# Attention products grouped by array mode: masks ahead of both halves, a mask as contraction rows, 64x64 products in runs

## The chip, the cores and the metric

The kernel runs on one core of a Trainium2 chip. The metric is device time in microseconds (us); a kernel's time is the median of its runs. TensorE (PE in the rows) multiplies, VectorE (DVE), ScalarE (ACT) and GpSimd (POOL) work on vectors, and SyncE (SP) issues the loads.

## The reference

A network of two kinds of layer, two layers of each, on 256 tokens of width 1024. A layer of the first kind has a feed-forward part, a token mixer with three branches (retention, latent attention, differential attention), cross attention to 256 memory tokens, and a second feed-forward part. A layer of the second kind has a mixer of stick-breaking attention and gated linear attention, and then 32 experts of which each token uses two. The parts that the change touches, cut to their products:

```python
# latent attention, 8 heads of 64 + 32; a query sees the chunks of 64 keys up to its own
sc = (einsum('bqhd,bkhd->bhqk', qn, k_nope) + einsum('bqhd,bkd->bhqk', qr, k_rope)) * scale
p = masked_softmax(sc, chunk_causal_mask(i, s))
# differential attention, 4 heads with two halves j of 64
sc = einsum('bqhjd,bkhjd->bhjqk', qb, k) * scale
p = masked_softmax(sc, chunk_causal_mask(i, s))
w = p[:, :, 0] - lam * p[:, :, 1]
# stick-breaking attention, 8 heads of 64, strictly causal
z = einsum('bhqd,bhkd->bhqk', q_blk, k) * scale
log_fail = where(before, -softplus(z), 0.0)
w = where(before, exp(log_sigmoid(z) + suffix_sum(log_fail)), 0.0)
# gated linear attention, 4 heads (64 wide keys, 128 wide values), chunks of 64
intra = einsum('bhnqk,bhnkv->bhnqv', where(causal, q_dec @ k_inv.T, 0.0), vc)
chunk_kv = einsum('bhnkd,bhnkv->bhndv', kc * exp(b_last - b), vc)
inter = einsum('bhnqd,bhndv->bhnqv', q_dec, prev)     # prev: the state before the chunk
```

## The kernel before

Tokens lie in two tiles of 128. Weights stream from memory in raw chunks of 1 MB and are split on ScalarE (line 272, the high half) and VectorE (line 274, the low half) into operands of one pass each; a dense product (mm3, lines 284 to 286) multiplies high by high, high by low and low by high, 512 columns at a time. Attention products instead take 32-bit operands as they are, and TensorE runs each of these as two passes.

Dense work and attention are interleaved by hand. The function dense emits six products for one k-tile and then calls tick, which lets the first task of each of two queues emit its next piece. A task is a generator that yields for how many ticks its next piece may wait. TensorE, ScalarE, VectorE and GpSimd run in the order in which the program is written; SP's loads alone are placed by a scheduler. PSUM has six banks for products (mm) and two for transposes and small results (tp).

In mix (the mixer of the first kind), heads_T transposes latent queries and keys into qT and kT, tiles of 128 rows of which 96 are used. latent_pairs takes two heads at a time: chunk_scores (lines 751 to 756) first multiplies two rows of constants, mrow, which puts a large negative number on the masked scores, and then adds the scores of queries 0 to 127 on keys 0 to 127 and of queries 128 to 255 on all keys. softmax2 follows, and weights_T transposes the result a few ticks later. diff_heads calls chunk_scores for the two halves j of a head; half j lies in rows 64 j to 64 j + 63 of dT. Retention (ret_pairs, lines 1041 and 1042) multiplies two heads in the same layout without a mask: both products of j = 0 are written first, then both of j = 1.

In mix2, stick works on two heads at a time. For each half j, line 1504 puts the mask in PSUM by multiplying the identity with maskb, and lines 1505 and 1506 add the scores, of 64 contraction rows. ScalarE then takes Abs (line 1509), Exp (1510) and Ln (1511), VectorE adds (1513), and three ticks after the scores TensorE sums over keys (1518, 1519); two Exp (1522) and the product with the values (1493, 1494) follow. attention runs stick on three pairs, then linear, then the fourth pair. linear multiplies queries and keys (line 1546), makes the chunks' key-value products (kv, line 1557) one chunk per tick, updates the states S on VectorE, and then writes the output go head by head: the product within a tile (line 1575, 128 rows) and then those with the states (line 1579, 64x64). Eight squares on ScalarE (437), copies (1587), a power on GpSimd (406) and a scaling (1591) follow.

Of the kernel before, what the change touches and what calls it, by code (L numbers as in the profile page):

```python
# [13 lines left out]
BF16 = mybir.dt.bfloat16  # L14
# [44 lines left out]
def constants():  # L59
# [13 lines left out]
    mrow = np.zeros((1, 512), np.float32)  # L73
    mrow[0, :64] = 1.0
    mrow[0, 128 + 64:128 + 128] = NEG
    mrow[0, 128 + 320:128 + 384] = NEG
    c["mrow"] = mrow
    same = (i[:, None] // CHUNK) == (i[None, :] // CHUNK)
# [81 lines left out]
class Stream:  # L160
    """The weights in the order of their use: loads run ahead as far as the raw buffers go, the splits into
    (hi, lo) as far as the split buffers go."""
# [21 lines left out]
    def slot(self, i):  # L184
        """the place of the next split, from raw i, or None"""
# [53 lines left out]
class Kernel:  # L239
# [8 lines left out]
    # ---------------------------------------------------------------- helpers  # L248
# [19 lines left out]
    def split(self, place, raw, c0, n, pool=False):  # L268
        """(hi, lo) of n <= 512 columns"""
        nc = self.nc  # L270
        hi, lo = place[:, :n], place[:, 512:512 + n]
        nc.scalar.activation(hi, raw[:, c0:c0 + n], AF.Copy)  # L272
        eng = nc.gpsimd if pool else nc.vector
        eng.tensor_tensor(out=lo, in0=raw[:, c0:c0 + n], in1=hi.bitcast(F32), op=ALU.subtract)  # L274
        return hi, lo
# [12 lines left out]
    # tasks are generators that emit a piece of work and yield for how long (in steps of dense) the next may wait  # L288
# [39 lines left out]
    def dense(self, keys, kt, n, lhs, outs, mid=None):  # L328
        """outs[t] ([128, n <= 512] in PSUM) = lhs @ w; the chunks of the weights hold kt k-tiles of n columns."""
# [12 lines left out]
    def staggered(self, keys, lhs):  # L342
        """run(t), for t = 0 and then 1, gives outs[t] = lhs @ w for two chunks of 4 k-tiles of 512 columns"""
# [19 lines left out]
    def dense_out(self, keys, lhs, tail, closing=None, mid=(), ada=None):  # L363
        """y[t][half] ([128, 512] in PSUM), chunks of 2 k-tiles of 1024 columns, and a function that emits what is
        left to do for t = 1 in the last tail splits"""
# [32 lines left out]
    def rstd(self, out, ms, eps=EPS, mul=1.0):  # L398
        """out = (mul * ms + eps) ** -0.5"""
# [13 lines left out]
    def new_h(self):  # L413
        """(hi, lo) of a feature-major operand [128, tile, 8, 128]"""
# [3 lines left out]
    def to_fm_g(self, src, dst, nk):  # L418
        """dst = (hi, lo) [128, nk, 128] of the transposes of src [128, nk * 128]"""
# [19 lines left out]
    def rstd2(self, out, ms, eps=EPS):  # L439
        """out = (ms[0] + ms[1] + eps) ** -0.5"""  # L440
# [17 lines left out]
    def pre_load(self, pre):  # L458
        """gain and shift"""
# [7 lines left out]
    def add_post(self, y, t, post, g, u, junk):  # L467
        """x += the normalised or gated y (two halves of 512 columns), in two steps"""
# [40 lines left out]
    def boundary(self, ys, rest, post, gp, gn, first=None, filler=None):  # L509
        """adds the last stage's output to x and gives the next stage's normalised input, feature-major, and the  # L510
        outputs of the next stage's first projection"""
# [52 lines left out]
    # ---------------------------------------------------------------- setup  # L564
# [33 lines left out]
    def setup_rope(self):  # L598
# [3 lines left out]
        self.mrow = cp.tile([1, 512], BF16, name="mrowb")  # L602

        yield 0
        with self.tc.tile_pool(name="ropew", bufs=1) as wp:
            mrow = self.A1("mrow")[0:1, 0:512]
# [37 lines left out]
    # ---------------------------------------------------------------- FFN  # L644
# [12 lines left out]
    def vectors_of(self, l, which):  # L657
        """the modulation vectors (layer, number) that are made beside an FFN"""
# [46 lines left out]
    # ---------------------------------------------------------------- token mixing  # L705
    def rope(self, x, heads, si, rot, tmpp):
        """rotates the first rot columns of the heads x [128, tile, heads, width] in place"""
# [15 lines left out]
    def evacuate(self, dst, ps):  # L723
        """dst [128, 2, 512] = both tiles of ps"""
# [3 lines left out]
    def copy(self, dst, src):  # L728
        """on the scalar and the vector engine in turn"""
# [6 lines left out]
    def transposes_g(self, dst, blocks, rows=128):  # L736
        """dst [rows, n, 128] = transposes of the n blocks [128, rows]"""
# [13 lines left out]
    def chunk_scores(self, ps, qf, kf):  # L751
        """ps [128, 384]: queries 0-127 on keys 0-127, queries 128-255 on keys 0-255, chunk-causal"""
        te = self.nc.tensor
        te.matmul(ps[:, 0:384], self.mrow[:, 0:128], self.mrow[:, 128:512], start=True, stop=False)
        te.matmul(ps[:, 0:128], qf(0, 128), kf(0, 128), start=False, stop=False)
        te.matmul(ps[:, 128:384], qf(128, 256), kf(0, 256), start=False, stop=True)

    def softmax2(self, ps, P, scale, sm):
        """P = exp(scale * (ps - max)) for two score sets ps[j] [128, 384]; returns 1 / sums [128, 4] (set, tile)"""
# [15 lines left out]
    def weights_T(self, P, wp):  # L775
        """[128 keys, 384] = (keys 0-127 x queries 0-255 | keys 128-255 x queries 128-255) of P [128, 384]"""
# [8 lines left out]
    def attend_tm(self, pt, v, h, o):  # L785
        """o [128, 2, 128] in PSUM = weights @ v for the queries of both tiles"""
# [6 lines left out]
    def branch_fm(self, o, wp):  # L793
        """(hi, lo) [128, 4, 256] of o [128, 2, 512], appended to out"""
# [6 lines left out]
    def head_norms(self, o_tp, o, ms, h):  # L801
        """o (SBUF) and its mean squares from PSUM o_tp [128, 2, 128]"""
# [15 lines left out]
    def mix(self, l, hT, ps, pre):  # L818
# [7 lines left out]
        with ExitStack() as es:  # L826
# [23 lines left out]
            # latent attention: norms  # L850
# [26 lines left out]
            # differential attention: scalars  # L877
# [9 lines left out]
            # latent attention: queries  # L887
# [16 lines left out]
            def heads_T(dst, src, name):  # L904
                for t in range(2):
# [8 lines left out]
            # latent attention: keys and values  # L914
# [21 lines left out]
            def latent_pairs():  # L936
                last = None
                for hp in range(5):
                    if hp < 4:
                        ps = self.mm("msc")  # L940
                        for j in range(2):
                            h = 2 * hp + j
                            self.chunk_scores(ps[j], lambda c0, c1: qT[:96, h, c0:c1], lambda c0, c1: kT[:96, h, c0:c1])
# [24 lines left out]
            # differential attention  # L968
            branch = {0: (mh, ml)}

            def diff_heads():
# [11 lines left out]
                for h in range(5):  # L983
                    if h < 4:
                        ps = self.mm("dsc")
                        for j in range(2):
# [1067 lines left out]
```

## Time and profile before

| what | before |
|---|---|
| median of 3 runs | 2297.43 us |
| lowest and highest run | 2295.17, 2300.14 us |
| span of the profiled execution | 2296.8 us |
| TensorE busy | 2161.8 us (94%) |
| VectorE, ScalarE busy | 1338.2 us (58%), 1084.0 us (47%) |
| first mixer's latent to differential scores, layers 1 and 2 | 279 to 362, 1047 to 1130 us |
| second mixer's stick and linear part, layers 1 and 2 | 1607 to 1668, 1979 to 2040 us |

The profile records one execution; of it only the span, from the first to the last instruction, is given. A busy share is an average over all stages, so the stretches around the edited places are read on their own. A record of TensorE has a start and a modelled end; since products are pipelined, ends overlap, and the distance between starts tells what one costs.

### The profile page before, as it was taken

To read this page: it belongs to the slowest core of one execution; us is meant where nothing else is said; L and a number is where in the kernel's file an instruction comes from. 1 tells how busy PE (TensorE), PEld (TensorE's weight loads), DVE (VectorE), ACT (ScalarE), POOL (GpSimd) and SP (SyncE) were. 2 spreads that over 40 slices of the span, in tenths; PEclk is the share of its full clock that TensorE was granted. 3 is DMA by queue.
4 is the path that set the end of the run, shared out by engine and by line. 5 is a ranking of instruction groups with operands and counts; after the bars stand their busy time and mean duration, and the time that the engine had idled before them with its cause. 6 is when DMAs were issued, how large, how long until landed. Compare 5 with 4: busy or idle time off the path is not lost. (4 is left out here: it accounts for less than half of the span.)

```text
span 2296.8 us, 28925 instructions
## 1 busy us (share of the span) xinstructions
PE 2161.8 (94%) x10684; PEld 1584.9 (69%) x10684; DVE 1338.2 (58%) x2419; ACT 1084.0 (47%) x2178; POOL 121.2 (5%) x115
## 2 busy tenths in 40 slices
PE   7999999999999999999999999999989877998885
PEld 6887877888787787777788878877764334765341
DVE  6876666765876777676678567766461115453111
ACT  5544666565544555466656555445641103752110
POOL 1001000000100100010000010002010001001000
PEclk9999999999999999999999999999989898998998
DMA  8865434553676676653345447766389998558998
GB/s 291 300 242 209 178 125 151 196 198 129 211 279 236 218 277 242 234 196 129 145 181 202 160 141 277 240 231 242 116 316 393 420 419 316 197 202 327 419 418 338
DMA packets 96230, 559.27 MB, mean 244 GB/s; under 512 B 11135, under 2 KB 13105, under 8 KB 43086
## 3 DMA queue, kind: packets, MB, share of 16 engines
q1 hardware_dynamic: 96078, 557.30, 65.5%
q8 instruction: 88, 1.44, 0.2%
q14 instruction: 64, 0.52, 0.1%
HBM read 556.16 MB, written 1.10 MB: 243 GB/s over the span
## 5 line engine op out<-in xcount | busy, mean ns | idle before, releaser
L274 DVE TENSOR_TENSOR hl<-raw,hl 128x512 fp32r<-128x512 f32 (+2 forms) x586 | 391.6, 684 | 122.7 <-ACT hl L272 115.5
L272 ACT ACTIVATE hl<-raw 128x512 fp32r<-128x512 f32 (+1 forms) x602 | 367.3, 628 | 198.7 <-PE gu L286 49.6
L274 DVE TENSOR_TENSOR pair<-raw,pair 128x512 fp32r<-128x512 f32 (+2 forms) x468 | 304.8, 692 | 127.4 <-ACT pair L272 122.5
L272 ACT ACTIVATE pair<-raw 128x512 fp32r<-128x512 f32 x484 | 276.9, 623 | 186.2 <-PE gu L286 70.3
L1898 PE MATMUL gu<-raw,xg 128*32 128x512 f32 x1024 | 142.1, 626 | 25.4 <-DMA raw<-w_gu 25.4
L284 PE MATMUL gu<-hl,hh 128*128 128x512 f32 x320 | 127.6, 399 | 0.0
L284 PE MATMUL gu<-pair,hh 128*128 128x512 f32 x320 | 127.5, 398 | 0.0
L286 PE MATMUL gu<-hl 128*128 128x512 f32 x320 | 126.5, 395 | 0.0
L285 PE MATMUL gu<-hl,hh 128*128 128x512 f32 x320 | 126.1, 394 | 0.0
L286 PE MATMUL gu<-pair,hl 128*128 128x512 f32 x320 | 125.1, 391 | 0.0
L285 PE MATMUL gu<-pair,hh 128*128 128x512 f32 x320 | 124.8, 390 | 0.0
L1295 DVE SCALAR_TENSOR_TENSOR ada<-raw,cact,ada 128x512 f32<-128x512 f32 x168 | 121.9, 745 | 0.0
L1898 PEld LDWEIGHTS gu<-raw,xg 128*32 128x32 f32 x1024 | 29.2, 111 | 101.8 <-DMA raw<-w_gu 52.7
L1886 PEld LDWEIGHTS gather<-P,u 128*128 128x128 f32 x512 | 71.5, 219 | 32.6 <-issue 23.5
L279 DVE TENSOR_TENSOR y<-dn,y 128x512 fp32r<-128x512 f32 x32 | 22.1, 692 | 110.4 <-ACT y L278 110.4
L1937 ACT ACTIVATE sil<-gu 128x256 f32<-128x256 f32 x16 | 6.1, 384 | 163.2 <-PE gu L1898 163.2
L443 POOL TENSOR_TENSOR rs<-rs_tmp,mhalf 128x1 f32<-128x1 f32 x44 | 25.6, 583 | 1081.0 <-DVE rs_tmp L442 1075.8
L1955 PE MATMUL dn<-raw,aT 128*32 128x512 f32 x512 | 73.5, 621 | 8.9 <-DVE aT L1947 3.6
L1886 PE MATMUL gather<-P,u 128*128 128x128 f32 x512 | 78.6, 310 | 1.6 <-DVE P L1874 1.6
L1938 DVE SCALAR_TENSOR_TENSOR sil<-sil,cs,gu 128x256 f32<-128x256 f32 x16 | 7.7, 480 | 121.3 <-ACT sil L1937 121.1
L284 PE MATMUL y<-hl,ah 128*128 128x512 f32 x184 | 72.6, 395 | 0.0
L284 PEld LDWEIGHTS gu<-pair,hh 128*128 128x128 f32 x320 | 60.1, 188 | 17.0 <-ACT pair L272 2.5
(670 smaller groups left out, 4776.8 us busy)
## 6 DMA issues: line engine op xcount, KB each, us to landing
raw<-w SPq DMA_DIRECT2D x131, 1024.0 KB
raw<-w_gu SPq DMA_DIRECT2D x98, 1024.0 KB
raw<-win SPq DMA_DIRECT2D x71, 1024.0 KB
raw<-w_dn SPq DMA_DIRECT2D x54, 1024.0 KB
raw<-w_ada SPq DMA_DIRECT2D x48, 1024.0 KB
raw<-w_gu SPq DMA_DIRECT2D x60, 512.0 KB
raw<-w_out SPq DMA_DIRECT2D x16, 1024.0 KB
raw<-cross_wkv SPq DMA_DIRECT2D x16, 1024.0 KB
```

Of the source, the lines that this page charges most:

```text
L272: nc.scalar.activation(hi, raw[:, c0:c0 + n], AF.Copy)
L274: eng.tensor_tensor(out=lo, in0=raw[:, c0:c0 + n], in1=hi.bitcast(F32), op=ALU.subtract)
L279: self.nc.vector.tensor_sub(lo, src, hi.bitcast(F32))
L284: te.matmul(out, xh, wh, start=start, stop=False)
L285: te.matmul(out, xh, wl, start=False, stop=False)
L286: te.matmul(out, xl, wh, start=False, stop=stop)
L443: self.nc.gpsimd.tensor_tensor(out=out, in0=tmp, in1=self.mhalf[:, 0:1], op=ALU.pow)
L1295: nc.vector.scalar_tensor_tensor(self.ada[:, c], w, act, self.ada[:, c], op0=ALU.mult, op1=ALU.add)
L1886: te.matmul(ps[:, (k - k0) * 128:(k - k0 + 1) * 128], hm[t][:, k * 128:(k + 1) * 128], P[t][:, q * 128:(q + 1) * 128], start=(t == 0), sto ...
L1898: te.matmul(gu[32 * e:32 * e + 32, :], xg[:, k, 32 * e:32 * e + 32], w(e), start=(k == 0), stop=(k == 7))
L1938: ve.scalar_tensor_tensor(sil, sil, cs[:, q:q + 1], gu[:, 256:512], op0=ALU.mult, op1=ALU.mult)
L1955: te.matmul(dn[half][32 * e:32 * e + 32, :], aT[:, f, 32 * e:32 * e + 32], w(e), start=(f == 0), stop=(f == 1))
```

## The change

Four things change. The latent mask becomes two more contraction rows: a constant mqk is loaded into rows 96 and 97 of qT and kT, the products have 98 rows, and no mask product is left. For differential attention, chunk_mask writes the masks of both halves first, over the masked columns alone, and the scores of both halves follow; the columns without a mask are not started first. In stick the masks of both halves stand first too, over 256 columns where it were 384. In linear, the key-value products of chunks 0 and 1 are emitted together, and the output has the eight products of 128 rows first and then the twelve of 64x64. The changed kernel also has comments and docstrings taken out, so its line numbers differ.

```diff
-    def chunk_scores(self, ps, qf, kf):
+    def chunk_mask(self, ps):
+        out = ps.rearrange("p (a b) -> p a b", a=2)[:, :, 64:128]
+        self.nc.tensor.matmul(out, self.mrow[:, 0:128], self.mrow[:, 128:256].rearrange("p (a b) -> p a b", a=2),
+                              start=True, stop=True)
+
+    def chunk_scores(self, ps, qf, kf, masked):
         te = self.nc.tensor
-        te.matmul(ps[:, 0:384], self.mrow[:, 0:128], self.mrow[:, 128:512], start=True, stop=False)
-        te.matmul(ps[:, 0:128], qf(0, 128), kf(0, 128), start=False, stop=False)
-        te.matmul(ps[:, 128:384], qf(128, 256), kf(0, 256), start=False, stop=True)
+        te.matmul(ps[:, 0:128], qf(0, 128), kf(0, 128), start=not masked, stop=True, skip_group_check=masked)
+        te.matmul(ps[:, 128:384], qf(128, 256), kf(0, 256), start=not masked, stop=True, skip_group_check=masked)
...
             def heads_T(dst, src, name):
+                rows = a["mqk"][("qT", "kT").index(name)].rearrange("r (h n) -> r h n", h=8)
+                nc.sync.dma_start(dst[96:98], rows)
...
-                            self.chunk_scores(ps[j], lambda c0, c1: qT[:96, h, c0:c1], lambda c0, c1: kT[:96, h, c0:c1])
+                            self.chunk_scores(ps[j], lambda c0, c1: qT[:98, h, c0:c1], lambda c0, c1: kT[:98, h, c0:c1],
+                                              False)
...
                         for j in range(2):
+                            self.chunk_mask(ps[j])
+                        for j in range(2):
                             r = slice(64 * j, 64 * j + 64)
-                            self.chunk_scores(ps[j], lambda c0, c1: dT[r, h, c0:c1], lambda c0, c1: dT[r, 4 + h, c0:c1])
+                            self.chunk_scores(ps[j], lambda c0, c1: dT[r, h, c0:c1], lambda c0, c1: dT[r, 4 + h, c0:c1],
+                                              True)
...
-        self.maskb = cp.tile([128, 384], BF16, name="maskb")
+        self.maskb = cp.tile([128, 128], BF16, name="maskb")
...
-        nc.gpsimd.memset(self.maskb, 0.0)
...
                 for j in range(2):
+                    te.matmul(ps[j].rearrange("p (a b) -> p a b", a=2)[:, :, 0:128], self.identb,
+                              self.maskb.unsqueeze(1).to_broadcast([128, 2, 128]), start=True, stop=True)
+                for j in range(2):
                     r = slice(64 * j, 64 * j + 64)
                     q, k = qk[r, hp, :], qk[r, 4 + hp, :]
-                    te.matmul(ps[j][:, 0:384], self.identb, self.maskb, start=True, stop=False)
-                    te.matmul(ps[j][:, 0:256], k[:, 0:128], q, start=False, stop=False)
-                    te.matmul(ps[j][:, 256:384], k[:, 128:256], q[:, 128:256], start=False, stop=True)
+                    te.matmul(ps[j][:, 0:256], k[:, 0:128], q, start=False, stop=True, skip_group_check=True)
+                    te.matmul(ps[j][:, 256:384], k[:, 128:256], q[:, 128:256], start=False, stop=True,
+                              skip_group_check=True)
...
+            kvs = []
             for c in range(3):
-                t, r = c // 2, slice(64 * (c % 2), 64 * (c % 2) + 64)
-                kv = self.tp("kv")
-                for hp in range(2):
-                    te.matmul(kv[:, hp * 256:(hp + 1) * 256], ex[2][r, t, hp * 128:(hp + 1) * 128],
-                              gv[r, t, hp * 256:(hp + 1) * 256], start=True, stop=True)
+                if c != 1:
+                    for c2 in ((0, 1), (2,))[c // 2]:
+                        t, r = c2 // 2, slice(64 * (c2 % 2), 64 * (c2 % 2) + 64)
+                        kvs.append(self.tp("kv"))
+                        for hp in range(2):
+                            te.matmul(kvs[c2][:, hp * 256:(hp + 1) * 256], ex[2][r, t, hp * 128:(hp + 1) * 128],
+                                      gv[r, t, hp * 256:(hp + 1) * 256], start=True, stop=True)
+                kv = kvs[c]
...
             for t in range(2):
                 for h in range(4):
-                    cs = slice(h * 128, (h + 1) * 128)
-                    j, pl = h % 2, place(t, h)
-                    te.matmul(ps[j][:, pl], sc[:, j, pl], gv[:, t, cs], start=True, stop=True)
-                    for c in (2 * t, 2 * t + 1):
-                        if c:
-                            r = slice(64 * (h % 2), 64 * (h % 2) + 64)
-                            te.matmul(ps[j][64 * (c % 2):64 * (c % 2) + 64, pl], qki[r, h // 2, c * 64:(c + 1) * 64],
-                                      S[r, h // 2, c - 1, :], start=False, stop=True, skip_group_check=True)
+                    te.matmul(ps[h % 2][:, place(t, h)], sc[:, h % 2, place(t, h)], gv[:, t, h * 128:(h + 1) * 128],
+                              start=(t == 0 and h < 2), stop=True, skip_group_check=True)
+            for hp in range(2):
+                for c in range(1, 4):
+                    for j in range(2):
+                        r, pl = slice(64 * j, 64 * j + 64), place(c // 2, 2 * hp + j)
+                        te.matmul(ps[j][64 * (c % 2):64 * (c % 2) + 64, pl], qki[r, hp, c * 64:(c + 1) * 64],
+                                  S[r, hp, c - 1, :], start=False, stop=True, skip_group_check=True)
```

TensorE's order at the first differential head: dsc is the bank of a half (two numbers, two halves), gate the dense product around it. Before:

```order
L286 MATMUL gate_2794<-hl 128x512
L754 LDWEIGHTS mrowb
L754 MATMUL dsc_2904<-mrowb 128x384
L755 MATMUL dsc_2904<-dT 128x128
L756 MATMUL dsc_2904<-dT 128x256
L754 LDWEIGHTS mrowb
L754 MATMUL dsc_2905<-mrowb 128x384
L755 MATMUL dsc_2905<-dT 128x128
L756 MATMUL dsc_2905<-dT 128x256
L284 MATMUL gate_2934<-hl,hh 128x512
```

And of the change:

```order
L290 MATMUL gate_2788<-hl 128x512
L759 LDWEIGHTS mrowb
L759 MATMUL dsc_2898<-mrowb 128x2x64
L759 LDWEIGHTS mrowb
L759 MATMUL dsc_2899<-mrowb 128x2x64
L765 MATMUL dsc_2898<-dT 128x128
L766 MATMUL dsc_2898<-dT 128x256
L765 MATMUL dsc_2899<-dT 128x128
L766 MATMUL dsc_2899<-dT 128x256
L288 MATMUL gate_2928<-hl,hh 128x512
```

The second half's mask has moved ahead of the first half's scores, so the four products of 64 rows stand together; stick-breaking pairs changed in the same way.

SP's order at the first mixer's start; gm and dl are its small constants, win, wq_b and wkv_b its weights. Before:

```order
L848 DMA dl<-dlam 128x256
L410 DMA gain<-g_mix 128x1024
L265 DMA raw<-win 128x2048 x2
L410 DMA gain<-g_cross 128x1024
L265 DMA raw<-wq_b 128x1536
L265 DMA raw<-win 128x2048 x2
L265 DMA raw<-wkv_b 128x1024
```

And of the change:

```order
L858 DMA dl<-dlam 128x256
L916 DMA qT<-mqk 2x2048
L269 DMA raw<-win 128x2048 x2
L916 DMA kT<-mqk 2x2048
L269 DMA raw<-wq_b 128x1536
L414 DMA gain<-g_mix 128x1024
L269 DMA raw<-win 128x2048 x2
L414 DMA gain<-g_cross 128x1024
L269 DMA raw<-wkv_b 128x1024
```

The two mask rows are loaded ahead of the weights that follow dl, and two gains have moved behind wq_b and win. Elsewhere the order changes only at the edited products and, among the experts, by four products that gather tokens.

## Rows read from the trace of the kernel before

**Rows 1.** Stretches: us, busy by engine (records), PEclk, DMA share, GB/s

```profile
330.00:360.00 30.00, 30.00 (x140) 21.87 (x138) 19.02 (x51) 23.00 (x57) 0.00 (x0) 1.00 0.34 118
1610.00:1630.00 20.00, 20.00 (x96) 14.13 (x94) 9.51 (x17) 17.42 (x27) 0.00 (x0) 1.00 0.38 140
1690.00:1710.00 20.00, 12.91 (x68) 11.00 (x66) 14.21 (x31) 8.29 (x17) 9.18 (x8) 0.67 0.91 350
```

**Rows 2.** Timeline, TensorE, first latent pair: start, length, line, out<-in, rows*columns, shape, records

```profile
278.46 0.39 PE L285 MATMUL rqk<-hl,hh 128*128 128x512 f32 x1
278.69 0.39 PE L286 MATMUL rqk<-hl 128*128 128x512 f32 x1
279.01 0.33 PE L754 MATMUL msc<-mrowb 1*128 1x384 bf16 x1
279.27 0.49 PE L755 MATMUL msc<-kT,qT 96*128 96x128 f32 x2
279.60 0.60 PE L756 MATMUL msc<-kT,qT 96*128 96x256 f32 x2
280.13 0.33 PE L754 MATMUL msc<-mrowb 1*128 1x384 bf16 x1
...
281.38 0.39 PE L285 MATMUL rqk<-hl,hh 128*128 128x512 f32 x1
```

**Rows 3.** Timeline, TensorE, first differential head

```profile
330.80 0.40 PE L286 MATMUL gate<-hl 128*128 128x512 f32 x1
...
333.35 0.50 PE L284 MATMUL gate<-hl,hh 128*128 128x512 f32 x1
333.69 0.40 PE L285 MATMUL gate<-hl,hh 128*128 128x512 f32 x1
```

**Rows 4.** Timeline, TensorE, first pair of retention heads

```profile
392.20 0.71 PE L1041 MATMUL rsc<-rT 64*128 64x256 f32 x4
392.73 0.40 PE L1042 MATMUL rsc<-rT 64*128 64x128 f32 x4
393.06 0.50 PE L284 MATMUL proj<-hl,brh 128*128 128x512 f32 x1
```

**Rows 5.** Timeline, all engines, first stick-breaking pair

```profile
1607.38 0.34 PE L1504 MATMUL sb<-maskb,identb 128*128 128x384 bf16 x1
...
1609.61 0.51 PE L284 MATMUL gqk<-hl,hh 128*128 128x512 f32 x1
1609.71 0.49 ACT L1509 ACTIVATE s<-sb 128x384 f32<-128x384 f32 x1 [0.62 <-PE sb L1506]
...
1613.36 1.02 DVE L1513 SCALAR_TENSOR_TENSOR s<-sb,s 128x384 f32<-128x384 f32 x2 [5.83 <-ACT s L1511]
...
1613.97 0.91 PE L1518 MATMUL sb<-s,tri 128*128 128x384 f32 x2
```

**Rows 6.** Tile sb: until what its engine sat idle before it (us, times)

```profile
  DVE s L1513: 1.4, 4
```

**Rows 7.** Timeline, TensorE, linear attention of layer 1 and behind it

```profile
1643.82 1.13 PE L1557 MATMUL kv<-gv,ex 64*128 64x256 f32 x4
1644.88 0.50 PE L284 MATMUL gr<-hl,hh 128*128 128x512 f32 x1
...
1649.02 0.39 PE L1575 MATMUL go<-gv,gsc 128*128 128x128 f32 x2
...
1652.44 0.44 PE L1579 MATMUL go<-S,qki 64*64 64x128 f32 x4
...
1655.16 0.50 PE L284 MATMUL gr<-hl,hh 128*128 128x512 f32 x1
...
1662.77 0.50 PE L285 MATMUL gr<-hl,hh 128*128 128x512 f32 x1 [0.60 <-DVE hl L274]
```

**Rows 8.** Timeline, SP's queue, first mixer's start

```profile
208.76 0.42 SPq L848 DMA_DIRECT2D dl<-dlam  x1
```

**Rows 9.** Waits of SP's queue: line, waited for, us in total, times, longest

```profile
SPq L1658 <- DMA raw<-w_gu: 88.6, 59, 2.3
```

More of the change, by code (lines that the diff above doesn't have):

```diff
@@ L72, in constants @@
     c["decay"] = (dec * 64 ** -0.5).astype(np.float32).reshape(128, RET_H * 384)
-    mrow = np.zeros((1, 512), np.float32)
+    mrow = np.zeros((1, 256), np.float32)
     mrow[0, :64] = 1.0
-    mrow[0, 128 + 64:128 + 128] = NEG
-    mrow[0, 128 + 320:128 + 384] = NEG
+    mrow[0, 128:256] = NEG
     c["mrow"] = mrow
+    mqk = np.zeros((2, 2, 8, 256), np.float32)
+    for r in range(2):
+        mqk[0, r, :, 128 * r:128 * r + 64] = 1.0
+        mqk[1, r, :, 128 * r + 64:128 * r + 128] = NEG
+    c["mqk"] = mqk.reshape(2, 2, 2048)
     same = (i[:, None] // CHUNK) == (i[None, :] // CHUNK)
@@ L601, in setup_rope @@
         nc.sync.dma_start(self.decay, a["decay"].rearrange("p (h n) -> p h n", h=RET_H))
-        self.mrow = cp.tile([1, 512], BF16, name="mrowb")
+        self.mrow = cp.tile([1, 256], BF16, name="mrowb")
         yield 0
         with self.tc.tile_pool(name="ropew", bufs=1) as wp:
-            mrow = self.A1("mrow")[0:1, 0:512]
+            mrow = self.A1("mrow")[0:1, 0:256]
             nc.sync.dma_start(mrow, a["mrow"])
@@ L1332, in rest @@
         def rest():
-            for c in (0, 256):
-                nc.vector.tensor_copy(self.maskb[:, c:c + 128], masks[:, 2, :])
+            nc.vector.tensor_copy(self.maskb, masks[:, 2, :])
             nc.vector.tensor_copy(self.beforeb, masks[:, 0, :])
```

## The prediction

> **What bounds the kernel now.** I first read busy time in stretches of the attention stages [rows 1]. From 330 to 360 us, inside the first kind of layer (function mix), TensorE is busy for 30.00 of 30.00 us, while ScalarE has 23.00 and VectorE 19.02. From 1610 to 1630 us, inside the second kind (mix2), it is busy for 20.00 of 20.00 us, but ScalarE is close behind with 17.42. The granted clock is 1.00 in both. So in mix a microsecond taken from TensorE is a microsecond of the program, as long as nobody else is late; in mix2 ScalarE's chains have to be looked at before that is said. The DMA engines are busy for 0.34 and 0.38 there, and 0.91 from 1690 to 1710 us, once the mixer's buffers have been given up: the stream of expert weights speeds up only after mix2, so a mix2 that ends earlier moves that stream forward too.
>
> Then I read TensorE's records in order of time around each edited place. A dense product of 512 columns starts 0.23 us after the one ahead (278.46 to 278.69). The mask product, which has one contraction row, starts 0.32 us after a dense one, so 0.09 us go where the array changes its number of rows or columns. The mask holds it for 0.26 us; its successor, a product of 128 columns, for 0.33 us, and the next, of 256 columns, until 280.13, that is 0.53 us [rows 2]. A 32-bit product runs as two passes; a pass of 128 columns takes 0.11 us, so the product takes 0.22 us, and 0.44 us at 256 columns (0.53 less the 0.09 of the next change). The 0.33 is then 0.22 and 0.11 of weight load that nothing hid. So a change of array shape costs about 0.20 us: 0.09 to empty, 0.10 or 0.11 for a bare weight load. Going from 96 rows to 128 costs nothing: the second mask begins at 280.13, and 0.26 + 0.33 + 0.44 us later, at 281.16, its products are through; the dense stream is back at 281.38 - 0.23 = 281.15.
>
> **Latent scores (8 pairs of heads: 4 in each of 2 layers).** Before, a pair lasts from 278.69 + 0.23 = 278.92 to 281.15, or 2.23 us [rows 2]. The change drops both masks and puts them into two more contraction rows. What is left is 2 x (0.22 + 0.44) = 1.32 us with no change of shape. That saves 0.91 us a pair, 7.3 us in all. I give the extra rows (98 for 96) no cost, since 64 and 96 rows fill the same places in time. They need four new DMAs of two rows each. These stand in SP's queue right behind the load of dl, issued at 208.76 us [rows 8]; the first product that reads them is at 279, so some 70 us hide them.
>
> **Differential scores (8 heads).** Before, a head lasts from 330.80 + 0.23 = 331.03 to 333.69 - 0.23 = 333.46, or 2.43 us, with five changes of shape [rows 3]. Now come both masks, then the four products of 64 rows. No row shows two masks in succession; 384 columns take 0.16 us without the change, so 128 take 0.05 at least, and the 0.26 us between a mask and its successor is the most. I take 0.08 for the first, near the lower end because the second has the same shape, and 0.05 + 0.10 for the second. For the rest there is an exact model: retention issues the same four products, first half 0, then half 1, with nothing between them. They occupy 0.86 us from 392.20 to 393.06, and all four passes of L1041 stand ahead of all four of L1042 [rows 4]: the halves, on different rows of the array, run side by side. So 0.09 + 0.08 + 0.15 + 0.86 + 0.11 (bare load of the next dense product) = 1.29 us. It saves 1.14 us a head, 9.1 us in all. Side by side both halves end late, so VectorE's maxima no longer run beside half 1, and the softmax is done some 0.7 us later after the scores. TensorE, busy for 30.00 of 30.00 us here, waits for no softmax now [rows 1], and I take the 0.7 as spare time; at worst it is a wait of 0.7 us in each of 8 heads, 5.6 us.
>
> **Stick-breaking scores (8 pairs of heads).** Before, a pair takes 1607.38 to 1609.61, or 2.23 us [rows 5]. Now two masks of 256 columns (0.12 each), a change (0.09 less what the block contains) and the block of 0.86: about 1.18 us. TensorE saves 1.05 us a pair, 8.4 in all. But this does not all stay. Half 0 used to be ready 1.1 us (half of 2.23) ahead of half 1, and ScalarE's first Abs ran beside half 1. Now both are ready together, and the chain Abs, Abs, Exp, table load, Ln, then VectorE's L1513, grows by one Abs, 0.49 us. L1518 begins at 1613.97, when VectorE's step, begun at 1613.36, has given its first half: there is no slack, and 4 of the 8 pairs waited for that step [rows 6]. Those 4 give back 0.49 us each, 2.0 us.
>
> **Linear attention (2 layers).** The visit for chunk 1 goes: 0.09 + 1.06 (1643.82 to 1644.88) + 0.11 = 1.25 us [rows 7]. Its products run beside chunk 0's, on the other 64 rows. They need the second of two PSUM banks, which the stick-breaking output ahead still holds for a moment, so I allow 0.45 us: 0.8 saved, 1.6 in all. The output takes 1649.02 to 1655.16 plus 0.11, or 6.25 us [rows 7]. Now the eight products of 128 rows come first, 8 x 0.22 = 1.79 us with the small gaps, then 0.09, then twelve of 64x64 on four tiles. Four products stand on the busiest tile, so 4 x 0.22 + 0.05 of bare load = 0.92, then 0.09 and 0.11: 3.0 us. The row with x4 at 1652.44 shows two column tiles that share 0.44 us; that four tiles do is not shown, and if only two did it would be 0.7 us more. It saves 3.25, 6.5 in all.
>
> Behind the output hangs a chain that ends at L285 at 1662.77, where TensorE waited 0.60 us for VectorE's low halves [rows 7]. ScalarE squares eight pieces of the output (0.40 us each), VectorE copies, GpSimd takes the power, VectorE scales and only then splits the weights. This chain starts at the output's end, so it moves with it; but the fourth stick-breaking pair lies inside it, and its 1.05 us become wait, 2.1 in all. And since both output banks are now ready only at the very end, all eight squares stand behind it and not seven: 0.40 us more, 0.8 in all.
>
> **Sum.** 7.3 + 9.1 + 8.4 + 1.6 + 6.5 = 32.9 us off TensorE, less 2.0 + 2.1 + 0.8 = 4.9 given back: 28.0 us. The profiled execution has a span of 2296.8 us, so 2268.8; the median of the three runs is 2297.43, 0.6 above it, and I put the forecast beside the median: 2269.4 us. The masks set up once (fewer columns, one memset less) I count at nothing; they lie on VectorE and GpSimd beside dense work.
>
> **The rivals.** *Halves do not overlap.* If products start strictly in the program's order, half 1 waits for half 0. Then each differential head and stick pair saves 0.66 less, the chunk visit saves only its changes of shape (0.39), and the twelve products take 2.7 us: 7.3 + 3.8 + 2.3 + 0.8 + 3.0 - 0.8 = 16.4, so 2281.0 us. Against it stand [rows 4]. The Trainium skill states this order (TensorE: Matmul & The Clock Gate, What overlaps and what doesn't: matmuls start and end in program order, only weight loads are pulled ahead); by it the result is this rival's 2281.0. The trace disagrees, with four passes of L1041 ahead of L1042 in 0.86 us. Chance 0.08.
>
> *ScalarE sets the pace of mix2.* With 17.42 of 20 us busy, all that TensorE saves there may become wait. Then only 7.3 + 9.1 = 16.4 us stay, again 2281.0. For it: every chain there passes ScalarE. Against it: only 4 of 8 pairs waited [rows 6], and the output's 3.25 us lie ahead of a chain that starts at its end. Chance 0.09.
>
> *Nothing is given back.* If the Abs finds other time and the tail chain shortens too, 32.9 and the 0.9 allowed at the chunk stay: 2263.6 us. Chance 0.04.
>
> *Slower: the expert loads.* The four new DMAs shift the turn of every later load among the DMA semaphores, and four products that gather expert tokens move. SP waits 59 times, 88.6 us in all, 1.5 us each, for a load of w_gu to land before it issues another [rows 9]. To undo 28 us each would have to grow by 0.47 us, and by 0.55 (1.5 to 2.05 us) to make the kernel 0.2% slower, 2302 us. Against it: a shift of all turns by the same number leaves the distance between loads. Chance 0.03.
>
> **How the numbers follow.** The forecast as worked out has 0.76. Its own bounds are the masks (up to 1.5 us more), the four tiles (1.4 more), the chunk (0.9 either way), the softmax (up to 5.6 more), a longer or shorter ScalarE chain (3 either way) and the runs' spread (2.5); not all come together: 2264 to 2277. To hold 8 in 10, the range goes on to nothing given back and to the two cases at 2281: 2263 to 2281. A measurement of this kernel can tell about 0.2% (4.6 us) from no change. Below 2292.8 lie the forecast and three rivals, 0.97 together; 0.02 of that goes to within 0.2%, for what I have not seen. So faster 0.95, the same 0.02, slower 0.03.
>
> **What would show it.** Latent products of 98 rows without a mask line between, and a pair of 1.32 us. In a differential head, the passes of both halves in one row each (x4), the head at about 1.3 us. The stick-breaking second half waits some 0.5 us for VectorE in the first two pairs of a layer. The output block takes 3.0 us, and the wait for the low halves behind it grows from 0.60 to about 2 us. The forecast is wrong if halves run one after the other, if TensorE shows waits in mix, or if the expert stages grow.

## The result and the profile after

The changed kernel takes 2272.11 us (median of four runs, 2269.22 to 2275.62) beside 2298.78 us of the kernel before: 26.7 us less by the medians; the ratio of the runs is 0.9888, 95% interval 0.9873 to 0.9902, which is 25.7 us. Forecast were 2269.4 us, 28.0 less, in a range of 2263 to 2281. The profiled execution has a span of 2273.8 us, 23.0 less than the one before; where the rest lies is told under the clock below.

The same two stretches as in [rows 1], shifted by what had been saved. Columns: us, busy by engine (records), granted clock, DMA share, GB/s.

```profile
323.50:353.50 30.00, 30.00 (x161) 23.43 (x160) 18.31 (x48) 23.43 (x57) 0.00 (x0) 1.00 0.40 138
1598.00:1618.00 20.00, 19.44 (x102) 13.69 (x101) 9.51 (x17) 17.87 (x29) 0.00 (x0) 1.00 0.43 156
```

In this stretch of mix TensorE is still busy all the time, so what it was spared there is the program's. In mix2 it is no longer: 0.56 us of 20 are waits.

TensorE's records at the first latent pair and the first differential head, beside [rows 2, 3] and with their columns:

```profile
279.83 0.38 PE L765 MATMUL msc<-kT,qT 98*128 98x128 f32 x2
280.05 0.60 PE L766 MATMUL msc<-kT,qT 98*128 98x256 f32 x2
280.49 0.39 PE L765 MATMUL msc<-kT,qT 98*128 98x128 f32 x2
280.71 0.60 PE L766 MATMUL msc<-kT,qT 98*128 98x256 f32 x2
...
329.20 0.28 PE L759 MATMUL dsc<-mrowb 1*128 1x128 bf16 x2
329.41 0.50 PE L765 MATMUL dsc<-dT 64*128 64x128 f32 x4
329.73 0.61 PE L766 MATMUL dsc<-dT 64*128 64x256 f32 x4
330.27 0.50 PE L288 MATMUL gate<-hl,hh 128*128 128x512 f32 x1
```

A latent product of 128 columns takes 0.22 us and one of 256 takes 0.44 with 98 rows as with 96: the two extra rows cost nothing. In the head all four passes of L765 stand ahead of L766, and from 329.41 to 330.27 the block lasts 0.86 us, as retention's did in [rows 4].

At the first stick-breaking pair (with ScalarE's Abs and Exp), and at the linear attention of layer 1, beside [rows 5, 7]:

```profile
1596.34 0.39 PE L1516 MATMUL sb<-maskb,identb 128*128 128x256 bf16 x2
1596.66 0.71 PE L1521 MATMUL sb<-qkT 64*128 64x256 f32 x4
1597.20 0.39 PE L1522 MATMUL sb<-qkT 64*128 64x128 f32 x4
1597.52 0.51 PE L288 MATMUL gqk<-hl,hh 128*128 128x512 f32 x1
1597.61 0.87 ACT L1526 ACTIVATE s<-sb 128x384 f32<-128x384 f32 x2 [1.85 <-PE sb L1522]
1598.52 0.85 ACT L1527 ACTIVATE s<-s 128x768 f32<-128x768 f32 x1
...
1627.80 1.86 PE L1577 MATMUL kv<-gv,ex 64*128 64x256 f32 x8
1629.60 0.50 PE L288 MATMUL gr<-hl,hh 128*128 128x512 f32 x1
...
1635.13 1.95 PE L1594 MATMUL go<-gv,gsc 128*128 128x128 f32 x16
1637.01 1.09 PE L1600 MATMUL go<-S,qki 64*64 64x128 f32 x24
1638.03 0.50 PE L288 MATMUL gr<-hl,hh 128*128 128x512 f32 x1
```

And before, ScalarE's Exp behind the second Abs of [rows 5], and the key-value products of chunk 0 (the next dense product starts at 1642.25):

```profile
1610.24 0.84 ACT L1510 ACTIVATE s<-s 128x768 f32<-128x768 f32 x1
...
1641.29 1.03 PE L1557 MATMUL kv<-gv,ex 64*128 64x256 f32 x4
```

The pair takes 1.18 us, and the output's products are through in 2.90 us. The key-value block takes 1.80 us (1627.80 to 1629.60), where chunk 0 alone took 0.96 before (1641.29 to 1642.25): its eight passes did not run side by side.

What TensorE waited for from 1585 to 1656 us (in total, times, longest):

```profile
PE gr L289 <- DVE hl L278: 1.9, 1, 1.9
PE sb L1535 <- DVE s L1530: 0.6, 2, 0.3
```

To size each part I took one and the same dense product in both traces, ahead of an edited place and behind it, and compared how far the changed kernel was ahead. A visit is a break of the dense stream for small products; the weight load that the dense product behind it can't hide belongs to it. Sums over both layers, in us:

| part | forecast | measured |
|---|---|---|
| latent pairs, 8 | 7.3 | 7.4 (0.92 or 0.93 each) |
| wait at the third latent pair of a layer | none | -1.7 |
| differential heads, 8 | 9.1 | 9.2 (1.15 each) |
| wait behind the last head, layer 2 | only as a bound | -0.6 |
| stick-breaking pairs, 8 | 8.4 | 8.4 (1.05 each) |
| given back at the first two pairs of a layer | -2.0 | -1.5 (0.37 each) |
| key-value products | 1.6 | 0.8 |
| output | 6.5 | 6.5 |
| wait behind the output | -2.9 | -2.7 |
| sum | 28.0 | 25.8 |

The two waits that were not in the sum, TensorE's rows with those of the engine waited for: the transposes behind the third latent pair of layer 1 (first as they were before, then in the changed kernel), and those of the last differential head of layer 2.

```profile
298.42 0.82 PE L779 MATMUL tp<-ident,mP 128*128 128x128 f32 x6
...
296.54 0.49 PE L789 MATMUL tp<-ident,mP 128*128 128x128 f32 x3
297.13 0.49 ACT L792 ACTIVATE pt<-tp 128x384 f32<-128x384 f32 x1 [0.45 <-PE tp L789]
297.68 0.55 PE L789 MATMUL tp<-ident,mP 128*128 128x128 f32 x3 [0.64 <-ACT pt L792]
...
1121.91 1.14 DVE L776 TENSOR_REDUCE mx<-dsc 128x1 f32<-128x128 f32 x4
1126.36 0.49 DVE L1013 SCALAR_TENSOR_TENSOR dP<-dP,rsum 128x256 f32<-128x256 f32 x1
1126.90 0.44 PE L789 MATMUL tp<-ident,dP 128*128 128x128 f32 x2 [0.35 <-DVE dP L1013]
```

In the kernel before, the six transposes of the third pair are one unbroken run. In the changed one the second three start only when ScalarE has copied the first three out: this points to one bank for both sets, where before they had two; the run with another bank, below, tests it. In the second case VectorE begins the maxima at 1121.91, 3.6 us after the scores of the head are through (1118.27), since its queue holds splits and retention's work first. In the kernel before it began them at 1130.00, beside the head's last scores, and was done 3.4 us ahead of the transposes. TensorE comes to this head 10.9 us earlier than before and VectorE only 8.1 us earlier, in this head as in the two ahead of it: what TensorE gains in each head uses up VectorE's slack.

### The profile page after: what moved, and what is told of

The parts are those of the page before. It is cut to its first block, busy times and chain, and to the rows that moved or that the text cites. A ratio compares the mean times of both kernels' runs of the same rounds, so it can differ in the third digit from the quotient of the medians.

```text
span 2273.8 us, 28903 instructions
## 1 busy us (share of the span) xinstructions
PE 2135.8 (94%) x10668; PEld 1572.8 (69%) x10668; DVE 1336.8 (59%) x2418; ACT 1081.9 (48%) x2178; POOL 120.9 (5%) x114
## 5 line engine op out<-in xcount | busy, mean ns | idle before, releaser
L1976 PE MATMUL dn<-raw,aT 128*32 128x512 f32 x512 | 78.6, 660 | 7.0 <-DVE aT L1968 3.6
```

Of the source, the lines that this page charges most:

```text
L1976: te.matmul(dn[half][32 * e:32 * e + 32, :], aT[:, f, 32 * e:32 * e + 32], w(e), start=(f == 0), stop=(f == 1))
```

## The experiments

**The parts apart.** Two kernels between the two: the kernel before with the latent and differential edits alone, and with the stick-breaking and linear edits alone.

> The kernel before with the latent and the differential part of the change alone. Theory (parts add; a microsecond off TensorE in the first mixer is a microsecond of the program, but for one wait of 0.86 us at the third latent pair of a layer and one of 0.6 behind the last differential head of layer 2): 7.4 + 9.2 - 1.7 - 0.6 = 14.3 us less than before, a ratio of 0.9938; the wait of the transposes behind the third pair's scores is there as in the whole change. Rival (the wait at the third pair comes with the other parts of the change, not with this one): 16 us less, and no wait there.

Measured: 2282.56 us, ratio 0.9940 (0.9923 to 0.9956). The first mixers save 7.42 and 6.82 us (7.42 ahead of the wait behind the last head of layer 2), and the wait at the third pair is there in both layers, 0.64 us each. The parts add, and the wait belongs to the latent and differential edits.

> The kernel before with the stick-breaking and the linear part of the change alone. Theory (as read from the changed kernel's trace): 8.4 off the pairs, 6.7 off the output, 0.6 off the key-value products, less 1.5 given back in the first two pairs of a layer and 2.7 in the wait behind the output: 11.5 us less than before, a ratio of 0.9950. Rival C (ScalarE sets the pace of the second mixer): no more than 2 us less than before, 0.999.

Measured: 2284.56 us, ratio 0.9951 (0.9934 to 0.9968). The second mixers save 5.75 and 5.74 us. ScalarE as the pace of all of mix2 is excluded at this size. By the table, the 6.7 and 0.6 of this theory are 6.5 and 0.8: the 0.10 us a layer of weight load behind the visit that went is the visit's and not the output's.

**Side by side, or only in fewer modes?**

```diff
-    r = slice(64 * j, 64 * j + 64)
+    r = slice(0, 64)
```

> The changed kernel, but the second half of each differential head and of each stick-breaking pair reads rows 0 to 63 as the first does, so that half 1 computes half 0's scores again: all four products of a block now use the same 64 rows of the array, in the same order, with as many columns and no change of array shape. Theory A (the halves run side by side because they lie on different rows): without that a block takes 2 x 0.66 = 1.32 us and not 0.86, some 0.5 us more in each of 8 heads and 8 pairs, 7 to 8 us in all: about 2280 us beside 2272. Rival (the gain is only that changes of array shape are gone; products start strictly one after the other): the blocks stay at 0.86 us, and the time at 2272 within 2 us.

TensorE's records of this kernel at the first differential head:

```profile
327.51 0.28 PE L759 MATMUL dsc<-mrowb 1*128 1x128 bf16 x2
327.72 0.48 PE L765 MATMUL dsc<-dT 64*128 64x128 f32 x2
328.05 0.59 PE L766 MATMUL dsc<-dT 64*128 64x256 f32 x2
328.48 0.38 PE L765 MATMUL dsc<-dT 64*128 64x128 f32 x2
328.70 0.59 PE L766 MATMUL dsc<-dT 64*128 64x256 f32 x2
329.23 0.50 PE L288 MATMUL gate<-hl,hh 128*128 128x512 f32 x1
```

The block takes 1.51 us (327.72 to 329.23) and not 0.86, in all heads and pairs 1.50; all passes of half 0 start before the first of half 1, as written. So 0.64 us of each block's gain are overlap, by the halves' different rows, and 0.5 (1.15 less 0.64) are changes of shape and mask columns, which no run takes apart. Theory A's 1.32 was 0.19 short: it left out a weight load that nothing hides (0.10) and the change of shape behind the block (0.09). The kernel's time, 4028.59 us, says nothing here: other scores route the tokens otherwise, and the program moves 1265 MB by DMA where the changed kernel moves 559.

**The same kernel again, and the clock.**

> The changed kernel once more, unaltered. In its first trace TensorE's granted clock fell to 0.5 for 3.41 us behind each of four waits in stages that the change does not touch (at 217.5, 582.8, 982.1 and 1347.3 us), where the kernel before shows two falls of 3.41 us and one of 6.83 in the same places (581.6, 1349.6, 1557.8). Theory D (the falls are a draw of where in time the wait lies, and cost 0.5 to 1.3 us each in one execution): the edited stages repeat within 0.05 us, and the number of falls before 1600 us may differ from five; the span is 2268 to 2275 us. Rival (the falls belong to the changed code): the same five falls at the same stages, and a span within 1 us of 2273.8.

Measured: 2272.46 us, ratio 0.9888 (0.9872 to 0.9905), span 2275.3. The edited stages repeat within 0.06 us, and the falls of the clock do not come at the same five places, so the rival is out; the span lies 0.3 us above theory D's range. A stretch between a feed-forward part and the next stage, where TensorE waits three times for a norm and for weights' low halves (1.10, 0.72 and 1.95 us); for the kernel before, the changed one, and the changed one again:

```profile
207.94:226.80 18.86, 14.93 (x67) 10.56 (x65) 14.96 (x21) 9.87 (x22) 6.55 (x6) 1.00 0.55 185
```

```profile
207.56:227.72 20.16, 16.07 (x66) 11.80 (x65) 14.90 (x21) 9.75 (x22) 6.56 (x6) 0.92 0.35 122
```

```profile
207.13:226.00 18.87, 14.89 (x66) 10.56 (x65) 14.97 (x21) 9.88 (x22) 6.57 (x6) 1.00 0.38 131
```

The same instructions take 18.86 us where the granted clock stayed at 1.00 and 20.16 where its mean was 0.92; which of the two it is changes from one execution of the same kernel to the next. In the first trace of the changed kernel four such stretches cost 3.7 us more than before (1.3, 0.9, 1.0, 0.5), and that, with what varies in the experts, is why its span shows 23.0 us and not 25.8. The Trainium skill (TensorE: Matmul & The Clock Gate, What's actually happening) says that one and the same kernel runs more or fewer of its first matmuls at the lower clock from run to run; these traces show such a difference in the middle of a kernel (0.92 and 1.00 in the same stretch).

**The wait behind the output.** The scaling of the output one tick later, and then also the squares on VectorE:

```diff
+            yield 1
             nc.vector.tensor_mul(v, v, grs.unsqueeze(3).to_broadcast([128, 2, 4, 128]))
             go.append(y)
             done("go")
-            yield 1
```

> The changed kernel, with the scaling of the linear output written one tick later, so that VectorE takes the low half of the next weights before it and does not stand behind GpSimd's power. In the changed kernel TensorE waits 1.94 us there for that low half. Theory W (the wait is VectorE's order): it goes. What then comes late is the sum of the fourth stick-breaking pair: its chain on ScalarE still stands behind the eight squares, ends at 1645.7, and VectorE's step after it gives its first half at about 1646.35, while TensorE would be there at 1645.2: a new wait of about 1.1 us, so that 0.85 us a layer stay, 1.7 us in all. Rival (the pair's chain has slack): 1.9 us a layer, 3.8 us.

```diff
-            for t in range(2):
-                for h in range(4):
-                    self.square_sum(gms[:, t, h:h + 1], ps[h % 2][:, place(t, h)], 128)
...
+            nc.vector.tensor_mul(sc, y, y)
+            nc.vector.reduce_sum(gms, sc.rearrange("p t (h e) -> p t h e", h=4), AX.X)
```

> As the run with the late scaling, and the eight squares of the linear output leave ScalarE: VectorE copies the output first, multiplies it with itself and sums (some 3.6 us of a VectorE that stood idle from 1638.1 to 1640.9). Theory W: the fourth pair's chain on ScalarE now begins as soon as its scores are there and ends 1 us earlier; both waits go but for some 0.2 us: 1.7 to 1.9 us a layer against the changed kernel, 3.4 to 3.8 us in all, about 2268.5 us. Rival (VectorE becomes late): the low half of the weights comes no earlier than before, because VectorE's square and sum take longer than ScalarE's, and less than 1 us stays in all.

Measured: 2270.57 and 2268.82 us, ratios 0.9882 (0.9854 to 0.9911) and 0.9875 (0.9843 to 0.9907). From the late scaling, the fourth pair's sum; from the other, VectorE's scaling and step, and the sum:

```profile
1643.86 0.91 PE L1535 MATMUL sb<-s,tri 128*128 128x384 f32 x2 [1.19 <-DVE s L1530]
```

```profile
1643.52 1.22 DVE L1612 TENSOR_TENSOR go<-go,grs 128x1024 f32<-128x1024 f32 x1 [1.53 <-POOL grs L410]
1644.66 1.01 DVE L1530 SCALAR_TENSOR_TENSOR s<-sb,s 128x384 f32<-128x384 f32 x2
1645.26 0.91 PE L1535 MATMUL sb<-s,tri 128*128 128x384 f32 x2 [0.84 <-DVE s L1530]
```

The 1.94 us went, and 1.19 came back one step on, as theory W had it: 0.75 us a layer stay. With the squares on VectorE it is 1.10, not 1.7: the scaling, waiting for GpSimd, still stood ahead of the pair's step in VectorE's queue. The medians, of two runs each, do not tell these kernels, or the next two, from the changed one; the stages of the trace do.

**Ln in halves.**

```diff
-                nc.scalar.activation(s1, s1, AF.Ln, bias=self.ones[:, 0:1])
+                for j in range(2):
+                    nc.scalar.activation(s1[:, j, :], s1[:, j, :], AF.Ln, bias=self.ones[:, 0:1])
```

> The changed kernel, with ScalarE's Ln of a stick-breaking pair in two halves, so that VectorE's step on half 0 begins one half of Ln earlier (0.44 us). In the changed kernel TensorE waits 0.3 us at the sum of the first two pairs of a layer and the visit is 0.37 us late. Theory G (the chain that grew by one Abs is what comes late there): both waits go, 0.37 us in each of 4 pairs, 1.5 us in all. Rival (VectorE's own queue is late): the waits stay at 0.3 us.

Measured: 2272.44 us, ratio 0.9890 (0.9862 to 0.9919). The first pair, all engines:

```profile
1598.32 1.12 ACT L1529 ACTIVATE s<-s,ones 128x384 f32<-128x384 f32 x2
1599.35 1.65 ACT L276 ACTIVATE hl<-raw 128x512 fp32r<-128x512 f32 x3
1599.58 0.91 PE L1536 MATMUL sb<-s,tri 128*128 128x384 f32 x2
1601.02 1.28 ACT L1540 ACT_TABLE_LOAD   x1
1602.32 0.87 ACT L1540 ACTIVATE s<-sb 128x384 f32<-128x384 f32 x2
1602.91 0.19 PEld L1507 LDWEIGHTS sbo<-s,sbv 128*64 128x64 f32 x2 [0.37 <-ACT s L1540]
```

Both theories miss. The waits at the sum are gone, so the chain through Ln was what came late there; but the 0.31 us are given back at the product with the values, which now waits for Exp, and the key-value visit behind it takes 0.19 us a layer more. Between Ln and Exp ScalarE splits three pieces of weights and loads a table (1.65 and 1.28 us), without a pause: in these pairs ScalarE does set the pace.

**Key-value products.**

```diff
-                if c != 1:
-                    for c2 in ((0, 1), (2,))[c // 2]:
+                if c != 2:
+                    for c2 in ((0,), (1, 2))[c]:
```

> The changed kernel, but the key-value products of chunks 1 and 2 are written together and not those of 0 and 1. Chunks 1 and 2 lie on different halves of the rows too, and by their tick both banks are free. In the changed kernel the block with chunks 0 and 1 takes 1.80 us where chunk 0 alone took 0.96: chunk 1's first product started 0.05 us after VectorE had emptied the bank of the stick-breaking output, when chunk 0 was through. Theory B (the two chunks did not run side by side because of that bank): chunk 0 goes back to 0.96, the visit with chunks 1 and 2 takes about what the visit with chunk 2 alone takes now (1.25 us); 0.84 us a layer, 1.7 us in all. Rival (such products of 256 columns do not pair): the visit grows by 0.88 us, and nothing is gained.

Measured: 2273.35 us, ratio 0.9894 (0.9866 to 0.9923); by the trace 0.2 us a layer. Chunk 0 went back to 0.96 us, but the visit with chunks 1 and 2:

```profile
1629.08 1.23 DVE L1585 COPY S<-kv 64x128 f32<-64x128 f32 x4
1629.83 1.72 PE L1577 MATMUL kv<-gv,ex 64*128 64x256 f32 x8
1631.48 0.50 PE L288 MATMUL gr<-hl,hh 128*128 128x512 f32 x1
```

VectorE copied chunk 0 out until 1630.31; chunk 2's passes, which need that bank, began at 1630.45. So a bank held this pair apart too, and whether they can run side by side was still open.

**Another bank, and all together.** The third pair's second transposes in a bank of the products' pool; and with that, chunks 1 and 2 one tick later, the squares on VectorE, and the scaling behind the fourth pair's step.

```diff
-                        pts = [self.weights_T(last[:, j, :], ptp) for j in range(2)]
+                        pts = [self.weights_T(last[:, j, :], ptp, tp) for j, tp in
+                               enumerate((None, self.bank("ptx") if hp == 2 else None))]
...
-                    for c2 in ((0, 1), (2,))[c // 2]:
+                    for c2 in ((0,), (1, 2))[c // 2]:
...
-            yield from stick((3,))
+            last = stick((3,))
+            d = next(last)
+            v = go[0].rearrange("p t (h e) -> p t h e", h=4)
+            nc.vector.tensor_mul(v, v, grs.unsqueeze(3).to_broadcast([128, 2, 4, 128]))
+            done("go")
+            yield d
+            yield from last
```

> The changed kernel with (1) alone: the third pair's second transposes in another bank. Theory (the two sets of transposes were given the same bank, and that alone is the wait): the 0.64 us of wait go, the six transposes stand in one run, and 0.86 us a layer, 1.7 in all, are saved. Rival (something else that ScalarE does late is waited for, one step on): the wait is seen at the product with the values two ticks later, and nothing is saved.

> The changed kernel with what the runs point to. (1) The third latent pair's second transposes go to a bank of the products' pool, so that they don't wait for ScalarE's copy of the first: 0.86 us a layer. (2) The key-value products of chunks 1 and 2 stand together one tick later than in the run that tried them, when VectorE has emptied chunk 0's bank: 0.84 us a layer. (3) VectorE makes the output's squares, and the scaling stands behind its step for the fourth stick-breaking pair: the 1.94 us of wait behind the output go, and at most 0.2 us come back at the pair's sum: 1.7 us a layer. Theory: 6.8 us less than the changed kernel, some 2265.5 us and a ratio to before of 0.986. Rival (ScalarE and VectorE hand each gain on to the next step, as Ln in halves did): no more than 3 us less, 0.9875.

> The changed kernel, unaltered, on the same chip beside the other two: 2272 us and a ratio to before of 0.989, with the edited stages within 0.05 us of its earlier traces.

Measured side by side: 2266.69, 2265.40 and 2273.22 us, ratios to before 0.9869 (0.9849 to 0.9889), 0.9865 (0.9844 to 0.9885) and 0.9896 (0.9880 to 0.9913). With the other bank alone, the transposes:

```profile
294.55 0.49 PE L789 MATMUL tp<-ident,mP 128*128 128x128 f32 x3
294.88 0.49 PE L789 MATMUL ptx<-ident,mP 128*128 128x128 f32 x3
```

The wait is gone and nothing comes later: 0.86 us a layer, so the shared bank was the whole wait. The rest of its 6.5 us beside the unaltered kernel lies by the traces in stages that this edit does not touch: 2.1 at the experts of layer 1 (see the end of the next section), the others where the granted clock differs. With all together, the key-value visit, and what TensorE still waited for from 1585 to 1656 us:

```profile
1627.09 1.14 PE L1584 MATMUL kv<-gv,ex 64*128 64x256 f32 x8
```

```profile
PE sb L1536 <- DVE s L1531: 0.9, 3, 0.3
```

Now the eight passes take 1.14 us and not 1.72: with both banks empty (VectorE was through with chunk 0's at 1626.20) the chunks run side by side. The second mixer of layer 1 gains 2.4 us over the changed kernel, 0.8 by the products and 1.6 by the tail. Edited stages together are 6.6 us shorter than in the changed kernel, near theory's 6.8 and beyond the rival's 3, and the medians differ by 7.8. From the kernel with the other bank alone the medians (2265.40 and 2266.69) do not tell it apart.

The unaltered kernel missed one thing that was expected of it: the end of its second mixer in layer 2, from the product behind the 1.94 us of wait on, takes 4.54 us and not 2.91 (the same products in the kernel run again, all at 1.00):

```profile
2010.44:2014.98 4.54, 4.54 (x14) 3.23 (x14) 2.68 (x5) 3.11 (x5) 0.00 (x0) 0.62 0.75 280
```

At 2010.8 the granted clock fell to 0.5. The same stands behind this wait in layer 1 of the runs with key-value products 1 and 2 and with Ln in halves, so in 3 of the 14 times that the kept traces show this wait of 1.94 us; each cost 1.6 us more. The forecast's price of that wait left this out.

## Why the prediction was right, and where its steps missed

*Removed and added products.* Right to 0.03 us a piece. A change of shape at 0.09 to empty and 0.10 or 0.11 for a bare weight load, two passes of 0.11 us for each 128 columns, and halves on different rows in 0.86 us: latent pair 0.92 for 0.91, head 1.15 for 1.14, pair 1.05 for 1.05. The output came out as forecast, 3.25 us a layer. That four tiles of 64x64 run at once had not been shown; the 24 passes, 8 on the busiest tile, take 1.02 us until the next dense product, where the working has 0.92 and 0.09.

*Rival "halves do not overlap".* Refuted by the kernel with both halves on the same rows, 1.51 for 0.86 us. The Trainium skill (TensorE: Matmul & The Clock Gate, What overlaps and what doesn't) has products start in the written order; here all passes of L765, those of half 1 too, start before half 0's L766, which is written ahead of half 1. The measurement decides against the page.

*Latent pairs.* The step that failed is that all of 0.91 a pair stays. The second transposes of the third pair got a bank that was still full, as the run with another bank shows; why they were given it, no run shows. Cost: 0.86 us in each layer, 1.7. The prediction's own sign of being wrong, waits in mix, did appear, at 2.3 of 16.6 us.

*Differential softmax.* "TensorE waits for no softmax now, and I take the 0.7 as spare time" held in seven of eight heads. In the eighth VectorE's queue was 3.6 us behind the scores, and TensorE lost 0.6 us. The spare time was not used up by halves that end together (0.7 us) but by TensorE's lead over VectorE, which grew head by head.

*Key-value products.* The visit was worth 1.24 us, near the 1.25 of the working, but the allowance of 0.45 for the bank should have been 0.83, a whole run of chunk 1 behind chunk 0: mis-sized by 0.4 a layer, 0.8 in all.

*What is given back.* 0.37 for 0.49 at a first or second pair. The chain did grow by an Abs, but 0.49 is the length of one record: two in a row take 0.87, and Exp starts 0.91 us behind the first of them (1597.61 to 1598.52) where it started 0.53 behind the last before (1609.71 to 1610.24), so the second costs 0.38. The waits in [rows 6] were of TensorE's weight loads, 0.35 us each; its products waited for nothing there before, but had no slack either. Behind the output 1.34 us a layer and not 1.45: there the mechanism (squares, power, scaling, split) was right, and the runs with the late scaling show that two chains lay side by side, since taking one wait away uncovered the other.

*Rival "ScalarE sets the pace".* Not at the size of the rival, since 5.75 us a layer stay in mix2; but the run with Ln in halves shows that it holds in the first two stick-breaking pairs of a layer, and that more saving there would need ScalarE.

*Slower by expert loads.* No sign of it in the medians. What is left open: at the experts of layer 1 the changed kernel's three traces lose 2.1 to 2.6 us against the trace before, kernels that differ from it only in the mixers lose nothing or gain up to 1.7. SP's waits for w_gu did not grow (88.6 us, 59 times, in the first of the three, as in [rows 9]), which speaks against the loads, and the mean granted clock there is 0.86 in these three traces and 0.87 to 0.90 in all others that route tokens alike; but two kernels at 0.87 lose nothing, so the cause stays open.

*The sum.* No luck of size was in it: the latent wait, the softmax and the key-value bank missed by 3.1 us in one direction, the smaller terms by 0.9 in the other, and 25.8 of 28.0 came.

## What to carry to other kernels

In a kernel like this one, price a visit of small products as its passes plus about 0.2 us for every change of array shape, and put products that use different rows or columns of the array next to each other: the overlap (0.64 us a block here) is worth more than the spared changes. Before counting such a saving, list for each bank who empties it and when, since a pair whose second bank is not empty yet runs one after the other and gains the spared changes alone (0.4 us a layer here, and 0.8 more once both banks were empty). Where an engine waits behind an in-order queue, follow the chain one step past the wait that goes: twice here the next step gave most of it back.

## What the runs showed of the hardware that had not been expected

Passes on four 64x64 tiles start some 7 ns apart, and 24 of them fit into 1.02 us. Two halves' products start out of the written order where their rows differ (half 1's first at 329.42, ahead of half 0's second at 329.73), and in that order where both lie on the same rows. One execution and the next of the same kernel differ by up to 1.3 us in one stage of 19 us; of the rows, the granted clock differs (mean 1.00 or 0.92). A single wait of 1.94 us was followed by the lower of the two clocks in 3 of 14 cases.
